# Third and fourth stretch of the second-level products joined, and two more such products, in a Winograd-tiled decoder layer

## The chip, the cores and the metric

The kernel runs on one core of one Trainium2 chip. The metric is the device time of one execution in microseconds (us), and lower is better. The time before is a median of three runs.

## The reference, cut to what matters

One layer of a hybrid decoder over 1024 rows of 1024 numbers, all in float32:

```python
h = rms_norm(x, norm_mix_g)
proj = einsum('bsd,dc->bsc', h, w_in)            # 1024 x 9232 weights
q, k, v, z_a, gk_low, cb, cc, xc, z_c, g_a, g_c = split(proj)
gk = log_sigmoid(gk_low @ w_gk2 + b_gk) / 16
o  = gla_chunked(q, k, v, gk)                     # gated linear attention, chunks of 64
y_a = (rms_norm(o) * silu(z_a)) @ w_branch_a
u   = causal_dwconv(cc * xc, conv_w)              # three taps
y_c = (cb * u * silu(z_c)) @ w_branch_c
merged = sigmoid(g_a + b_ga) * y_a + sigmoid(g_c + b_gc) * y_c
x = x + merged @ w_out
x = x + sigmoid(rms_norm(x) @ w_ple_gate) * (p @ w_ple_proj)
return rms_norm(x, norm_final_g)
```

Nearly all of the work is products of 1024 x 1024 operands. The ones that matter here are h with the columns of q and k, and h with the columns of cc, xc, z_c and cb (the convolution branch).

## The kernel before, in words

**Products.** Every large product is tiled by Winograd's form of Strassen's method: two by two blocks, seven block products (numbered k = 0 to 6) in place of eight. A `Cell` is one such tile: 256 columns of weights against all of h, out as four blocks of 128 x 512. The names are q0, k0, q1, k1 (two heads each) and cc0 to cc3, xc0 to xc3, zc0 to zc3, cb0 to cb3. Each block product has four steps of contraction, and in each step float32 is made of three passes (`mm3`): the operand is split into a rounded part, "hi", and the rest, "lo", and TensorE computes hi·hi, hi·lo and lo·hi. So one block product is 12 matmuls of 128x512. ScalarE makes the hi parts (CAST) and VectorE the lo parts (a subtraction). The prepared weights live in a ring of `RING` = 6 hi and 6 lo buffers.

A cell holds three PSUM banks: X, Y and V. X takes products 0 and 3, V takes 1 and 5, Y begins as a copy of X (ScalarE) and takes 2, then 4, then 6. Cells run in pairs, the first on banks m0 to m2 and the second on m3 to m5, in the order 0, 1, 2, 3, 5, 4, 6, each number for both cells in turn. The finished blocks go to the cell's consumer: `q_cons` and `k_cons` multiply them by exponentials of the decays into a tile `Q` or `kk` and store that; the convolution's consumers gate them.

**Second level.** A `Deep` takes one block product, the same k of both cells of a pair, and tiles these two again by the same method: seven products of two contraction steps, each of 6 matmuls of 128x256, in place of 2 x 12 matmuls of 128x512. It runs in four stretches: the first is 6 matmuls (operand A into the left half of the first cell's bank, copied by ScalarE to the left half of the second cell's), the second is 12 (operand S, both banks), the third is 6 (operand T, the second bank's left half), the fourth is 18 (A and T into the first bank, then B into the second). Between the second and the third stretch, and between the third and the fourth, 256 columns of PSUM are added to other halves by VectorE, with the help of tiles `dw` that ScalarE copies out. The right operands, quarter sums of h, are called `turned0` (for k=0) and `turned1` (k=1) and are loaded once each; the fourth of them is written over a quarter of h's own tile.

Names such as zc1cb10 read: the pair zc1 and cb1, k = 0. A last letter A, S, T or B with hi or lo is the operand of the Deep.

**What sets the order.** `line_up` writes one list of the products of all pairs, and puts the stretches of a pair's Deeps into the list between the last products of the pair before. TensorE follows this list word for word; only attention's matmuls are slipped in. Everything else is recorded first (`Flow.note`) and then put in order by a planner (`put_in_order`), which takes for each engine the ready instruction with the earliest due time; `nc.hurry` makes the due time earlier by so many microseconds. The order is then fixed: each engine, and SyncE's queue of DMAs, works through its own list without overtaking.

**The places of the change.** Before, k = 0 is second-level in the pairs q0k0, q1k1 and all eight convolution pairs (two for each of the four groups), and k = 1 in all convolution pairs but the first, cc0xc0. q0k0 is special (`joined`): its first-level products 1 and 5 come ahead of the Deep, and product 2 begins a bank of its own, which `join` adds to X later. The pool `tq` holds `turned0`, the pool of the convolution stage (`vp`) held `turned1`. `Q` and `kk` have two buffers each. The rest of the kernel (embedding product, v and z_a, gates, attention, the three output projections) has no edit of its own, save that its four Deeps of k = 1 use the same code.

## Time and profile before

| | |
|---|---|
| median of three runs | 1063.58 us (1063.55 to 1064.24) |
| the profiled execution | 1063.67 us, its span 1061.9 us |
| TensorE matmul | 1052.7 us busy, 99% of the span, 5223 instructions |
| VectorE | 937.3 us busy, 88% |
| ScalarE | 671.1 us busy, 63% |
| DMA | 287.53 MB, 271 GB/s on average |
| granted TensorE clock | 0.999 |

The stage of q and k runs from about 227 to 310 us of the span and the convolution's from there to about 600 us. Matmuls are pipelined: the record of one 128x512 matmul is about 0.39 us long, but the next starts 0.23 us later, so prices here are taken from start to start. A row of the timeline has the start, the length, the engine, the source line (always that of the helper, 508), the operation, out<-in, shapes, and in brackets the idle time ahead of it with what ended it.

### The profile page before, as it was taken

The numbers are of one execution on the slowest core, as the hardware profiler recorded it, in microseconds if no ns is written. First come the engines' busy times: TensorE is split into PE (matmuls) and PEld (weight loads), VectorE is DVE, ScalarE is ACT, GpSimd is POOL, SyncE is SP. The second block draws the span as 40 slices with busy tenths as digits, with TensorE's granted clock in tenths as the row PEclk, the third lists the DMA queues.
The fourth block names the chain that finished last, engine by engine and source line by source line (L and its number), as shares of the span: only waits on it lengthen the run. The fifth ranks groups of instructions, "written<-read, shape, count | busy, mean of one in ns | idle before, by whom it ended". The sixth has DMA issues, their size and how long they took to land.

```text
span 1061.9 us, 16352 instructions
## 1 busy us (share of the span) xinstructions
PE 1052.7 (99%) x5223; PEld 894.0 (84%) x5223; DVE 937.3 (88%) x1595; ACT 671.1 (63%) x1282; POOL 52.0 (5%) x83
## 2 busy tenths in 40 slices
PE   9999999999999999999999999999999999999997
PEld 7888887888888888888888899988888888888886
DVE  6899869989988889889889897997999989899897
ACT  6867765776555556567566486776856545456655
POOL 0000000000000000000000011210000000012221
PEclk9999999999999999999999999999999999999999
DMA  9997679878877766876869789988686979799963
GB/s 320 335 362 242 229 250 343 302 252 289 279 216 242 262 215 197 269 251 223 293 221 324 247 258 333 326 265 324 214 295 215 324 218 325 245 325 326 318 214 143
DMA packets 182726, 287.53 MB, mean 271 GB/s; under 512 B 16112, under 2 KB 84976, under 8 KB 180208
## 3 DMA queue, kind: packets, MB, share of 16 engines
q1 hardware_dynamic: 182496, 286.23, 79.5%
q8 instruction: 41, 0.67, 0.3%
q14 instruction: 45, 0.37, 0.1%
q10 hardware_dynamic: 144, 0.26, 0.1%
HBM read 183.14 MB, written 103.28 MB: 270 GB/s over the span
## 4 chain that ended last, share of the span: by engine, by line
PE 97%; DVE 1%; ACT 1%; DMA 0%; issue 0%; POOL 0%; POOLq 0%; SPq 0%; DVEq 0%
PE pe L508 2%; PE op L508 2%; PE zY L508 2%; PE j0Y L508 1%; PE vY L508 1%; PE zV L508 1%; PE j1V L508 1%; PE j1X L508 1%; PE j0V L508 1%; PE j0X L508 1%; PE kv L508 1%; PE ga0Y L508 1%; PE ga2Y L508 1%; PE xc2Y L508 1%; PE cc2Y L508 1%; PE cb1Y L508 1%
## 5 line engine op out<-in xcount | busy, mean ns | idle before, releaser
L508 DVE SCALAR_TENSOR_TENSOR u<-t,vec,u 128x512 f32<-128x512 f32 x32 | 23.9, 754 | 1.6 <-ACT u L508 1.5
L508 DVE TENSOR_TENSOR wt<-wt 128x256 f32<-128x256 f32 (+1 forms) x48 | 24.5, 511 | 0.1
L508 ACT ACTIVATE junk<-x 128x512 bf16<-128x512 f32 (+1 forms) x30 | 18.0, 600 | 10.0 <-DVE x L508 9.7
L508 POOL TENSOR_SCALAR rg<-ms 128x1 f32<-128x1 f32 x8 | 10.2, 1273 | 259.1 <-ACT junk L508 259.0
L508 POOL MEMSET t<- 128x2 f32 x8 | 0.8, 100 | 402.9 <-PE xc0V L508 210.1
L508 ACT ACT_TABLE_LOAD x13 | 16.7, 1283 | 0.9 <-PEq L2321 0.7
L508 ACT ACTIVATE og<-op,or 128x256 f32<-128x256 f32 x32 | 13.4, 474 | 4.2 <-DVE szl L508 2.1
L508 ACT ACTIVATE wt<-wt,vec 128x256 f32<-128x256 f32 x32 | 14.1, 499 | 1.4 <-DVE s L508 0.8
L508 ACT ACTIVATE junk<-op 128x256 bf16<-128x256 f32 x32 | 12.3, 383 | 2.1 <-PE op L508 2.0
L508 POOL TENSOR_SCALAR or<-oms 128x2 f32<-128x2 f32 x16 | 7.9, 494 | 115.7 <-ACT junk L508 115.7
L508 POOL TENSOR_TENSOR or<-or,consts 128x2 f32<-128x2 f32 x16 | 13.5, 842 | 1.3
L508 ACT ACTIVATE u<-t,vec 128x512 f32<-128x512 f32 x16 | 11.6, 723 | 3.0 <-DVE t L508 3.0
L508 ACT ACTIVATE oq<-oq,vec 128x512 f32<-128x512 f32 x20 | 13.4, 717 | 0.0
L508 PE MATMUL op<-v,aTh 128*128 128x256 f32 x64 | 12.9, 284 | 0.0
L508 PE MATMUL pe<-wpehi,pThi 128*128 128x512 f32 x32 | 12.6, 394 | 0.2 <-ACT pThi L508 0.2
L508 DVE TENSOR_TENSOR s<-y,s 128x512 f32<-128x512 f32 x16 | 11.0, 688 | 2.0 <-ACT s L508 1.8
L508 PE MATMUL pe<-wpelo,pThi 128*128 128x512 f32 x32 | 12.7, 397 | 0.0
L508 DVE STREAM_TRANSPOSE oT<-szl 128x256 f32<-128x256 f32 x32 | 12.6, 425 | 0.0
L508 PE MATMUL pe<-wpehi,pTlo 128*128 128x512 f32 x32 | 12.0, 389 | 0.0
L508 ACT CAST S<-S 128x512 fp32r<-128x512 f32 x14 | 8.6, 617 | 5.2 <-PE op L508 4.6
L508 DVE TENSOR_TENSOR x<-x,pe 128x512 f32<-128x512 f32 (+1 forms) x18 | 11.2, 630 | 0.3
L508 DVE SCALAR_TENSOR_TENSOR hq<-hq,vec,rt 128x512 f32<-128x512 f32 x16 | 11.3, 745 | 0.0
(4335 smaller groups left out, 4398.5 us busy)
## 6 DMA issues: line engine op xcount, KB each, us to landing
wtd<-wt SPq DMA_DIRECT2D x88, 128.0 KB, 3.0
wt<-in_wb_dram SPq DMA_DIRECT2D x16, 512.0 KB, 5.3
vsd<-vs SPq DMA_DIRECT2D x16, 512.0 KB, 4.4
v<-vsd SPq DMA_DIRECT2D x16, 512.0 KB, 5.4
vraw<-in_wv_dram SPq DMA_DIRECT2D x28, 256.0 KB, 4.9
wgq<-wtd SPq DMA_DIRECT2D x7, 1024.0 KB, 6.3
zraw<-in_wv_dram SPq DMA_DIRECT2D x20, 256.0 KB, 4.6
uq<-ud SPq DMA_DIRECT2D x5, 1024.0 KB, 7.7
```

The source lines that it names most:

```text
L508: o.call(*[place(a) for a in o.args], **{k: place(a) for k, a in o.kw.items()})
```

## The change

It has five parts.

1. Two more Deeps: k = 1 in the pair q1k1 and in cc0xc0.
2. `line_up` places them otherwise. In a convolution pair there were seven stretches of 128x256 matmuls with other products between; now the fourth stretch follows the third at once, in both Deeps, which leaves five. The same goes for the other pairs of q, k and convolution.
3. In a Deep, one `dw` copy in place of two: ScalarE copies the first bank's right half; VectorE adds it to the second bank's left half, once into the first bank's right half (after the second stretch) and once into the second bank's right half (after the third). These three instructions get 6 us of hurry.
4. q0k0 loses `join`: its order is now the Deep's first stretch, products 1 of both, 5 of the first, the second stretch, 5 of the second, third and fourth stretch, then 3, 2, 4, 6. Y is copied from X after the fourth stretch. Whichever of product 2 and product 5 comes last adds them (`finish`).
5. Memory: `Q` and `kk` share three buffers instead of two each; `turned1` moves to a new pool `tq1`, open from the q and k stage on, and is loaded there; the loads of `turned0` are all recorded at the start.

```diff
-        def join(self):
-            self.c12 = self.taken("u2", self.X)
-            tt(self.c12, self.Y, self.c12, op=ALU.add)
-            nc.scalar.copy(self.Y, self.c12)
+        def finish(self):
             tt(self.c12, self.V, self.c12, op=ALU.add)
             self.cons(0, 1, self.c12)
...
                 self.product(4, self.a[:, right], False)
                 self.product(2, self.b[:, left], False)
-                self.d = [self.pool.tile([P, 256], F32, tag=f"dw{n}", name=f"{a.name}{self.k}dw{n}") for n in range(2)]
-                nc.scalar.copy(self.d[0], self.b[:, left])
-                nc.scalar.copy(self.d[1], self.a[:, right])
-                tt(self.a[:, right], self.a[:, right], self.d[0], op=ALU.add)
+                self.d = self.pool.tile([P, 256], F32, tag="dw", name=f"{a.name}{self.k}dw")
+                nc.hurry = 6.0
+                nc.scalar.copy(self.d, self.a[:, right])
+                tt(self.a[:, right], self.b[:, left], self.d, op=ALU.add)
+                nc.hurry = 0.0
             elif k == 2:
                 self.product(1, self.b[:, left], False)
-                tt(self.b[:, right], self.b[:, left], self.d[1], op=ALU.add)
+                nc.hurry = 6.0
+                tt(self.b[:, right], self.b[:, left], self.d, op=ALU.add)
+                nc.hurry = 0.0
...
-                for n, m in enumerate((3,5,7,8)):
+                for n, m in enumerate((0,4,6,7)):
...
-                for m, (k, n, left) in enumerate(((0, 0, 5), (0, 1, 4), (0, 2, 3), (0, 3, 2), (1, 0, 2), (1, 1, 1), (1, 2, 0))):
+                for m, (k, n, left) in enumerate(((0, 0, 4), (0, 1, 3), (0, 2, 2), (0, 3, 2), (1, 0, 2), (1, 1, 1), (1, 2, 0), (1, 3, 0))):
                     todo.insert(at - left + m, (g[0].deep[k], n))
-                own.insert(1, (g[0].deep[1], 3))
...
-                Q = qp.tile([P, NP, 4, CH], F32, tag="Q", name=f"Q{nm}", bufs=2)
+                Q = qp.tile([P, NP, 4, CH], F32, tag="Qk", name=f"Q{nm}", bufs=3)
...
-            for g in convs[1:] if k else pairs(qks) + convs:
+            for g in (pairs(qks)[1:] if k else pairs(qks)) + convs:
                 Deep(g, k, turned[k], tq)
...
-            c.prods, c.joined = [1, 5, 2, 3, 4, 6], True
+            c.prods, c.joined = [1, 5, 3, 2, 4, 6], True
```

In the lists as built, TensorE has 48 matmuls of 128x512 fewer (3949 to 3901) and 84 of 128x256 more (1194 to 1278). VectorE has 14 additions or subtractions of 128x256 more (221 to 235); ScalarE 17 copies of 128x256 fewer (64 to 47), two casts of 128x512 and two of 128x256 more, and two loads of its function table fewer (13 to 11).

The first place is TensorE at the third stretch of zc1cb10, which writes the left half of cb1's bank X (its last three matmuls head each piece). Before:

```order
L508 MATMUL cb1X<-turned0h,zc1cb10Thi 128x256
L508 MATMUL cb1X<-turned0l,zc1cb10Thi 128x256
L508 MATMUL cb1X<-turned0h,zc1cb10Tlo 128x256
L508 MATMUL xc1Y<-h4hi,xc1hi 128x512
L508 MATMUL xc1Y<-h4lo,xc1hi 128x512
L508 MATMUL xc1Y<-h4hi,xc1lo 128x512
```

And now:

```order
L508 MATMUL cb1X<-turned0h,zc1cb10Thi 128x256
L508 MATMUL cb1X<-turned0l,zc1cb10Thi 128x256
L508 MATMUL cb1X<-turned0h,zc1cb10Tlo 128x256
L508 MATMUL zc1X<-h0hi,zc1cb10Ahi 128x256
L508 MATMUL zc1X<-h0lo,zc1cb10Ahi 128x256
L508 MATMUL zc1X<-h0hi,zc1cb10Alo 128x256
```

The product 4 of xc1, 12 matmuls, stood between the third and the fourth stretch; now the fourth stretch begins at once. Its last six matmuls write cb1's left half again, after VectorE has read it.

The second place is VectorE at that reading, the addition `cb1X<-cb1X,zc10dw`. Before:

```order
L508 TENSOR_TENSOR zc1cb11S_4677<-zc1T_4608,cb1T_4651 128x256
L508 TENSOR_TENSOR qs_3_4529<-qs_3_4529 128x2x128
L508 TENSOR_TENSOR cc1s_4471<-cc1Y,cc1s_4471 128x512
L508 TENSOR_TENSOR cb1X<-cb1X,zc10dw_4640 128x256
L508 SCALAR_TENSOR_TENSOR u_0_4683<-t_0_1_4056,vec,u_0_4683 128x512
```

And now:

```order
L508 TENSOR_TENSOR zc1cb11S_4776<-zc1T_4664,cb1T_4697 128x256
L508 TENSOR_TENSOR zc1cb11S_4781<-cb1T_4697 128x256
L508 TENSOR_TENSOR zc1cb11Alo<-zc1T_4664,zc1cb11Ahi 128x512
L508 TENSOR_TENSOR cb1X<-cb1X,zc10dw 128x256
L508 TENSOR_TENSOR zc1cb11S_4781<-zc1cb11S_4781,zc1T_4664 128x256
```

The addition now stands right behind `zc1cb11Alo`, the lo part of the next Deep's operand A, which itself needs ScalarE's cast `zc1cb11Ahi`.

The third place is ScalarE at q0k0, at the copy that begins the bank q0Y. Before:

```order
L508 CAST q1k10Ahi<-q1raw_2629 128x512
L508 COPY q0u_2795<-q0X 128x512
L508 COPY k0u_2807<-k0X 128x512
L508 ACTIVATE kk_0_2812<-cd_0_2693 128x4x2x64
L508 ACTIVATE kk_0_2812<-c_0_2671 128x4x64
L508 COPY q0Y<-q0u_2795 128x512
```

And now:

```order
L508 CAST q0hi<-q0T_2604 128x512
L508 CAST k0hi<-k0T_2610 128x512
L508 ACTIVATE kk_0_2617<-cd_0_2654 128x4x2x64
L508 COPY q0Y<-q0X 128x512
L508 CAST q1k10Ahi<-q1raw_2642 128x512
L508 COPY k0Y<-k0X 128x512
```

The copy reads q0X itself, and product 3 of q0, which follows the fourth stretch at once, adds into q0X.

More of the change, by code (lines that the diff above doesn't have):

```diff
@@ L828, in run @@
                 self.c22 = self.taken("s5", self.V)
-            elif k == 2 and self.joined:
-                self.Y = bank(self, 1)
-                self.product(2, self.Y, True)
-                if self.X is not None:
-                    self.join()
             elif k == 2:
@@ L836, in run @@
                 self.c12 = self.taken("u2", self.Y)
+                if self.summed:
+                    self.finish()
                 if self.halves:
@@ L844, in run @@
                 self.product(5, self.V, False)
+                self.summed = True
                 if self.c12 is not None:
-                    tt(self.c12, self.V, self.c12, op=ALU.add)
-                    self.cons(0, 1, self.c12)
+                    self.finish()
             elif k in (4, 6) and self.halves:
@@ L940, in run @@
                 self.product(6, self.b[:, left], False)
+                nc.hurry = 0.0
                 for c, t in ((a, self.a), (b, self.b)):
@@ L946, in run @@
                         c.X = t
-                    if c.joined:
-                        if c.Y is not None:
-                            c.join()
-                    elif 1 not in c.deep:
+                    if 1 not in c.deep:
                         c.Y = bank(c, 1)
@@ L954, in run @@
                         c.after(self.k)
+                nc.hurry = 0.0
     def line_up(groups):
@@ L978, in line_up @@
                 at = len(todo)
-                for n in range(3):
-                    todo.insert(at - 3 + 2 * n, (g[0].deep[0], n))
-                own.insert(1, (g[0].deep[0], 3))
+                for n, left in enumerate((3, 2, 1, 0)):
+                    todo.insert(at - left + n, (g[0].deep[0], n))
             elif g[0].deep:
@@ L1657 @@
     tq = phase("tq", [ph["v"]])
-    with phase("qk", [ph["v"]], tq) as qp:
+    tq1 = phase("tq1", [ph["v"]], tq)
+    with phase("qk", [ph["v"]], tq1) as qp:
         ex = lambda o, i_, sg: act(o, i_, AF.Exp, scale=sg / 16.0)
@@ L1814, in convolve @@
         def convolve():
-            weave(quarters(1), 1)
             weave(parts(), 16)
             weave(weights(vp, pieces[3:], 7, 60.0), 10)
-        weave(quarters(0), 1)
+        for _ in quarters(0):
+            pass
+        weave(quarters(1), 4)
         convs[0][0].begin = convolve
@@ L1939 @@
     ycs = [Cell(f"yc{c}", "B", W[f"yc{c}"], ures, None) for c in range(4)]
-    with phase("att", [ph["conv"]], tq) as ap:
+    with phase("att", [ph["conv"], tq1], tq) as ap:
         trim = ap.tile([P, P], I32, name="trim")
```

8 lines of the change are left out of this document (4 added, 4 removed).

## The prediction

> **What bounds the kernel now.** I read the page first: the busy shares, the granted clock, the chain that ended last.
>
> ```profile
> PE 1052.7 (99%) x5223; PEld 894.0 (84%) x5223; DVE 937.3 (88%) x1595; ACT 671.1 (63%) x1282; POOL 52.0 (5%) x83
> PEclk9999999999999999999999999999999999999999
> PE 97%; DVE 1%; ACT 1%; DMA 0%; issue 0%; POOL 0%; POOLq 0%; SPq 0%; DVEq 0%
> ```
>
> TensorE is busy for 99% of the span at full clock, and 97% of the chain is TensorE. So the time is TensorE's list, and an edit counts by how it changes that list or makes it wait. A busy share of matmuls can hide short waits, since their records overlap; so I took the two stages that the change touches from the windows view (busy us of PE, PEld, DVE, ACT, POOL, then clock, DMA share and GB/s), and then TensorE's rows from start to start.
>
> ```profile
> 226.96:310.00 83.04, 83.04 (x425) 71.12 (x424) 76.39 (x153) 50.02 (x98) 0.00 (x0) 1.00 0.85 269
> 310.00:330.00 20.00, 20.00 (x94) 16.72 (x93) 12.63 (x21) 9.87 (x20) 0.20 (x2) 1.00 0.88 290
> ```
>
> In q and k (227 to 310 us) VectorE is idle for 6.7 us and ScalarE for 33; in the next 20 us VectorE is idle for 7.4. Now TensorE's rows in q and k: the first matmul of six blocks, and one that comes 45 wide matmuls after the sixth.
>
> ```profile
> 264.18 0.28 PE L508 MATMUL k1X<-turned0h,q1k10Thi 128*128 128x256 f32 x1
> ...
> 264.89 0.40 PE L508 MATMUL k0Y<-h6hi,k0hi 128*128 128x512 f32 x1
> ...
> 267.63 0.39 PE L508 MATMUL q1V<-h1hi,q1hi 128*128 128x512 f32 x1
> ...
> 270.36 0.28 PE L508 MATMUL q1X<-h0hi,q1k10Ahi 128*128 128x256 f32 x1
> ...
> 272.51 0.40 PE L508 MATMUL k1V<-h1hi,k1hi 128*128 128x512 f32 x1
> ...
> 275.25 0.39 PE L508 MATMUL q1Y<-h2hi,q1hi 128*128 128x512 f32 x1
> ...
> 285.45 0.39 PE L508 MATMUL k1X<-h3hi,k1hi 128*128 128x512 f32 x1
> ```
>
> A wide matmul (128x512) costs (285.45 - 275.25) / 45 = 0.2267 us, a narrow one (128x256) (272.51 - 270.36) / 18 = 0.1194. Twelve wide ones behind a narrow stretch take 272.51 to 275.25 = 2.74 us (264.89 to 267.63 likewise), against 12 x 0.2267 = 2.72: a return from narrow to wide costs about 0.02.
>
> **The two more Deeps, and fewer stretches.** TensorE loses 48 wide matmuls and gains 84 narrow ones: -48 x 0.2267 + 84 x 0.1194 = -10.88 + 10.03 = -0.85 us. In the list, q, k and convolution have 62 blocks of wide matmuls before and 49 now: 13 returns fewer, -13 x 0.02 = -0.26. Together -1.11 us, all of it on the bounding engine, with nothing beside it that could hide it.
>
> [...]
>
> **The work that the Deeps add elsewhere.** VectorE gets 14 operations of 128x256 more:
>
> ```profile
> 241.62 0.43 DVE L508 TENSOR_TENSOR q0X<-q0X,q00dw 128x256 f32<-128x256 f32 x1
> 241.95 0.42 DVE L508 TENSOR_TENSOR q1k10S<-q1raw,k1raw 128x256 f32<-128x256 f32 x1
> ...
> 264.85 0.69 DVE L508 TENSOR_TENSOR k1lo<-k1T,k1hi 128x512 fp32r<-128x512 f32 x1 [0.17 <-ACT k1hi L508]
> ```
>
> They cost 0.33 us each from start to start (the first two rows), so 4.6 us, against the 14.1 us (6.7 + 7.4) idle above. The third row shows the cover: `k1lo` is done at 265.5, and k1's product 1, which needs it, begins at 272.51, 7 us later. ScalarE's copies fall by 17. Cost on the path: nothing as long as that lead lasts; without any idle time and lead it would be the 4.6 us.
>
> **The joint of third and fourth stretch.** This is the edit that can cost. Before, at least one whole product (2.72 us) stood between the two in q1k1 and the convolution pairs; now the third stretch's six matmuls into the second cell's left half are followed by twelve narrow ones (1.43 us) and then by six that add into that same left half, which VectorE must have read by then. Behind the waiting matmuls the rest of TensorE's list is queued, so every bit of lateness is lost time. The trace has such joints already: in ga2ga3 and in q0k0.
>
> ```profile
> 651.37 0.28 PE L508 MATMUL ga3V<-turned2h,ga2ga31Tlo 128*128 128x256 f32 x1
> ...
> 652.81 0.28 PE L508 MATMUL ga2V<-h1hi,ga2ga31Tlo 128*128 128x256 f32 x1
> 653.03 0.39 PE L508 MATMUL ga3V<-h1hi,ga2ga31Bhi 128*128 128x256 f32 x1
> 653.26 0.28 PE L508 MATMUL ga3V<-h1lo,ga2ga31Bhi 128*128 128x256 f32 x1
> ```
>
> ```profile
> 651.95 0.69 DVE L508 TENSOR_TENSOR szl<-og,szl 128x512 f32<-128x512 f32 x1
> 652.56 0.42 DVE L508 TENSOR_TENSOR ga3V<-ga3V,ga21dw 128x256 f32<-128x256 f32 x1
> ...
> 243.67 0.43 DVE L508 TENSOR_TENSOR k0X<-k0X,q00dw 128x256 f32<-128x256 f32 x1 [0.51 <-PE k0X L508]
> ```
>
> ```profile
> 243.35 0.28 PE L508 MATMUL k0X<-turned0h,q0k00Tlo 128*128 128x256 f32 x1
> ...
> 244.91 0.28 PE L508 MATMUL k0X<-h0hi,q0k00Bhi 128*128 128x256 f32 x1
> ```
>
> In q0k0 VectorE was free: the addition starts 243.67 - 243.35 = 0.32 us after the third stretch's last matmul started, ends at 0.75, and the B matmul comes on time at 1.56. In ga3 VectorE was inside `szl`: the addition started at 1.19, ended at 1.61, and B came 0.05 later, at 1.66. From 652.81 to 653.26 it takes 0.45 us where two narrow matmuls take 0.24: 0.21 lost. So the addition may start up to about 1.07 us after the last T matmul: 0.75 us of delay is free, more than the 0.60 of one wide operation ahead of it, less than two.
>
> What stands ahead of it now? In eight of the nine second-level products of k = 0 that get this joint new, the lo part of the next Deep's A, which waits for ScalarE's cast, which waits for the ring buffer that the wide product before the third stretch sets free. Such a cast and lo part, with that product's last matmul:
>
> ```profile
> 374.91 0.39 PE L508 MATMUL cb0Y<-h4hi,cb0lo 128*128 128x512 f32 x1
> ```
>
> ```profile
> 375.16 0.62 ACT L508 CAST cc1xc11Ahi<-cc1T 128x512 fp32r<-128x512 f32 x1 [1.62 <-PE cb0Y L508]
> ```
>
> ```profile
> 375.93 0.69 DVE L508 TENSOR_TENSOR cc1xc11Alo<-cc1T,cc1xc11Ahi 128x512 fp32r<-128x512 f32 x1
> ```
>
> Count from the wide product's end, E = 374.91 + 0.23 = 375.14: the lo part starts at E + 0.79, the addition behind it at E + 1.39 and ends at E + 1.82. B is due at E + 0.72 (third stretch) + 1.43 = E + 2.15 and wants the end by E + 2.10: 0.28 us to spare. So an ordinary joint is free, and one with a second hold-up ahead costs up to the 0.21 of ga3. There are 18 new joints (nine for k = 0, nine for k = 1). Bounds: 0 and 18 x 0.21 = 3.8 us. I take 0.3, near the lower end, as VectorE's row nearest to the new order leaves room and the additions get hurry.
>
> The same edit could give something back: the ga3 joint also gets the hurry, up to -0.21; I take 0.
>
> **The copy that begins q0Y.** In q0k0, product 3 of q0 follows the fourth stretch at once and adds into q0X, and the copy q0Y<-q0X must be done first. q0X is complete six narrow matmuls (0.72 us) before that product. Prices: ScalarE's release and a wide copy.
>
> ```profile
> 239.17 0.28 PE L508 MATMUL q0X<-turned0h,q0k00Slo 128*128 128x256 f32 x1
> ```
>
> ```profile
> 239.49 0.37 ACT L508 COPY q00dw<-q0X 128x256 f32<-128x256 f32 x1 [0.32 <-PE q0X L508]
> ...
> 245.62 0.58 ACT L508 COPY q0u<-q0X 128x512 f32<-128x512 f32 x1
> ```
>
> From q0X's last matmul 0.32 to the copy, 0.58 for it, 0.05 back: 0.95, against 0.12 + 0.72 = 0.84. So 0.11 us is lost at the least, and 0.10 for the restart as in ga3. ScalarE has `kk`'s exponential just ahead in its order, which adds up to another 0.5. Bounds 0.2 and 0.8; I take 0.4, nearer to the lower end, since the copy waits in the order for that one exponential only.
>
> **The start of q and k.** The Deep's operands now come first in the ring, so VectorE does A, S, T and B of q0k0 before `q0lo`.
>
> ```profile
> 219.98 0.68 DVE L508 TENSOR_TENSOR j641lo<-zT,j641hi 128x512 fp32r<-128x512 f32 x1
> 220.58 0.69 DVE L508 TENSOR_TENSOR vbase<-j6X,vbase 128x512 f32<-128x512 f32 x1
> ...
> 226.96 0.39 PE L508 MATMUL q0V<-h1hi,q0hi 128*128 128x512 f32 x1
> ```
>
> Between `j641lo` and `q0lo` stand 11 wide operations and one narrow: 219.98 + 12 x 0.60 + 0.33 = 227.5 to start, 228.2 to end. TensorE wants it with the third matmul behind the first stretch: 226.96 + 0.72 + 0.45 = 228.1. Bounds 0 and 0.3; I take 0.1. `turned0` is wanted earlier too:
>
> ```profile
> 226.79 0.58 SPq L508 DMA_DIRECT2D turned0h<-tqd_0h  x1
> ...
> turned0h<-tqd_0h SPq DMA_DIRECT2D x1, 256.0 KB, 4.9
> ```
>
> Issued at 226.8 it lands 4.9 us later, at 231.7, and the second stretch now starts at 226.96 + 0.72 + 3 x 2.72 = 235.8: 4 us of cover, so no cost; the change would have to delay the load by as much.
>
> **Sum.** -1.11 + 0.3 + 0.4 + 0.1 = -0.3 us. The profiled execution (1063.67) would come to 1063.4. It lies 0.09 above the median, so the median comes to 1063.3.
>
> **Rivals.** First, *all gain, no wait*: every joint and the copy find their engines free but for the 0.2 of the copy, and ga3's 0.21 goes: -1.11, so 1062.5; with the copy free too, 1062.3. For it: q0k0's joint, on time with 0.75 to spare. Against it: the copy's 0.95 against 0.84.
>
> Second, slower: *the addition is late at every joint*. If a second wide operation, 0.60, gets in ahead at each one, the addition ends at E + 2.42 and B loses 0.32 us; at some 0.30 over 18 joints that is +5.4, so 1063.58 - 1.11 + 5.4 = 1067.9. It decides from 0.18 us per joint on (3.2 us in all). For it: in ga3 it happened, with VectorE 88% busy. Against it: it must happen nearly everywhere. [...]
>
> Third, *the shared buffers*: `Q` and `kk` now come free after three consumers and not four, that is one product, 2.72 us, sooner wanted.
>
> ```profile
> ACT Q L508 <- DMA qkd<-Q: 2.1, 2, 1.7
> ...
> ACT kk L508 <- DMA qkd<-kk: 1.0, 1, 1.0
> ...
> qkd<-Q SPq DMA_DIRECT2D x8, 512.0 KB, 4.2
> ```
>
> ScalarE waited for such stores already (the first two rows, from the waits of 227 to 320 us); a store lands after 4.2 us. Two waits that outlast everything by 1.5 us (4.2 - 2.7) would give +3.0 - 0.3: 1066.3. Against it: ScalarE has 33 us idle there, and the casts behind the wait lead TensorE by many us. DMA, at 0.85 of its share, also takes the 2 MB of `turned1` earlier.
>
> That the change doesn't do what it says is no rival: TensorE's list has the 48 and 84.
>
> **How the numbers follow.** A measurement of this kernel tells about 0.2%, 2.1 us, from no change. Forecast (new waits of 0.3 to 2.2 us, 1062.8 to 1064.7): 0.76, no change. All gain: 0.11, no change as well, since even 1.3 us is under the bound. Late additions: 0.07, slower. Buffers: 0.04, half of it slower. Something unseen that gives over 2.1 us: 0.02. So faster 0.02, same 0.89, slower 0.09. The range takes in the forecast, the all-gain case and a little of the buffers' case: 1062.2 to 1065.0.
>
> **What would show it.** Right: blocks of 18 and 24 narrow matmuls merged into 24 and 30; TensorE's rows at the k = 0 and k = 1 joints without gaps over 0.2 us; a gap of 0.2 to 0.6 us ahead of q0X<-h3hi near 243 us. Wrong: gaps at most B matmuls, waits of TensorE on `cb1X` and its like in every pair, or casts that wait for `qkd` stores with TensorE idle behind them; and a time under 1061.4 or over 1065.7.

## The result and the profile after

The changed kernel takes 1065.89 us (median of 22 runs, 1064.56 to 1067.82), the kernel before 1064.01 in the same sets of runs (22 runs, 1063.41 to 1064.96). The ratio is 1.0018, with a 95% interval of 1.0012 to 1.0025: 1.9 us slower. That is just inside the 0.2% within which the prediction spoke of no change, but the interval excludes that there is no difference, and 1065.89 lies above the forecast range (1062.2 to 1065.0). Of the 2.6 us between forecast and result, 0.43 is the kernel before itself, whose 22 runs lie that much above the three shown earlier; 2.2 is the change. The spread from lowest to highest has also grown, from 1.5 to 3.3 us. Among the experiments' runs below, two single executions stand far out (1508.69 us of the kernel before, 3577.39 us of x6) and are left out of the ratios. Two executions of the changed kernel were profiled, one near its fast end (1064.80, span 1062.8) and one near its slow end (1067.14, span 1065.1).

Busy time and chain of the page, changed kernel:

```profile
PE 1052.5 (99%) x5259; PEld 894.9 (84%) x5259; DVE 941.8 (89%) x1609; ACT 666.7 (63%) x1267; POOL 49.0 (5%) x83
PE 94%; DVE 3%; ACT 2%; issue 1%; DMA 1%; POOL 0%; SPq 0%; POOLq 0%; DVEq 0%; ACTq 0%
```

TensorE's share of the chain is 94%, before 97%: there are now waits on VectorE and ScalarE that end last. Where they are is told by TensorE's waits (engine and line, what it waited for, us in total, times, longest). Two rows are new, the rest is as before:

```profile
PE cc0Y L508 <- ACT cc0Y L508: 0.5, 1, 0.5
...
PE q0X L508 <- ACT q0Y L508: 0.2, 1, 0.2
```

The copy `q0Y` was foreseen, `cc0Y` was not. Smaller waits than these hide in the overlap of the records, so I again took TensorE's rows from start to start and counted as a gap what a step takes beyond 0.2267 us (wide) or 0.1194 (narrow). Gaps in us, by place:

| | q0k0 with the start | end of q and k, with cc0xc0 | rest of the convolution | sum |
|---|---|---|---|---|
| changed, first profile | 0.78 | 0.91 | 0.40 | 2.09 |
| changed, second profile | 0.80 | 2.06 | 0.87 | 3.73 |

Five first starts in the three traces give the other side of the account:

| us | before | changed, first | changed, second |
|---|---|---|---|
| to j6Y, the last block ahead of q and k | 219.02 | 218.89 | 219.62 |
| j6Y to xc0Y<-h6hi | 125.75 | 126.73 | 127.88 |
| xc0Y to zc3Y<-h6hi | 252.43 | 252.56 | 253.02 |
| zc3Y to gc1Y<-h6hi | 122.39 | 122.32 | 122.32 |
| gc1Y to the last matmul | 334.41 | 334.41 | 334.41 |

In the first profile q and k grew by 0.98 with 1.69 of gaps, so the shorter list gave 0.71 there; the convolution grew by 0.13 with 0.40 of gaps, so 0.27. Together about 1.0 us of the 1.11 came. The gaps took 2.1 to 3.7. So the account is -1.0 + 2.1 = +1.1 for the first profile (measured 1064.80 against 1063.67, +1.13) and -1.0 + 3.7 = +2.7 for the second (measured 1067.14, +3.47). Of the 0.8 us that the second account misses, 0.60 lies ahead of j6Y (219.62 against 219.02), outside the stages that the change touches, and the rest outside the span (1067.14 - 1065.1 against 1063.67 - 1061.9).

**The end of q and k.** Here is the wait for `cc0Y`, followed back in the timeline of the changed kernel:

```profile
299.31 0.68 DVE L508 TENSOR_TENSOR Q<-q1s,Q 128x512 f32<-128x512 f32 x1
304.86 0.42 DVE L508 TENSOR_TENSOR Q<-Q,dcs 128x256 f32<-128x256 f32 x1
305.34 0.52 SPq L508 DMA_DIRECT2D qkd<-Q  x1
310.05 0.62 ACT L508 CAST cc0hi<-cc0raw 128x512 fp32r<-128x512 f32 x1 [1.97 <-PE k1Y L508]
310.57 0.63 ACT L508 ACTIVATE Q<-c 128x512 f32<-128x512 f32 x1
312.08 0.68 DVE L508 TENSOR_TENSOR Q<-q1Y,Q 128x512 f32<-128x512 f32 x1
312.92 0.28 PE L508 MATMUL xc0V<-h1hi,cc0xc01Blo 128*128 128x256 f32 x1
313.13 0.57 ACT L508 COPY cc0Y<-cc0X 128x512 f32<-128x512 f32 x1
313.75 0.50 PE L508 MATMUL cc0Y<-h2hi,cc0hi 128*128 128x512 f32 x1 [0.55 <-ACT cc0Y L508]
314.08 0.39 PE L508 MATMUL cc0Y<-h2lo,cc0hi 128*128 128x512 f32 x1
```

and the same steps before:

```profile
302.40 0.68 DVE L508 TENSOR_TENSOR Q<-q1Y,Q 128x512 f32<-128x512 f32 x1
306.86 1.20 SPq L508 DMA_DIRECT2D qkd<-Q  x2
310.18 0.59 ACT L508 COPY cc0Y<-cc0X 128x512 f32<-128x512 f32 x1
```

cc0's new bank Y is the bank of q1Y, so the copy waits until VectorE has read q1Y. Read the first fence backwards: that reading (312.08) needs the exponentials of a new `Q` tile (310.57). They need a buffer, which the store at 305.34 frees. That store waits for the multiplication by `dcs`, which stands at 304.86 although its input was done at 299.99: for the most part operands of cc0xc0's new second-level product stand ahead of it in VectorE's order. The store lands 3.2 us after its issue, at 308.56, so the buffer is free 2.0 us before the exponentials start. What they wait for last is their turn on ScalarE, behind the cast `cc0hi` (310.05), which stands 1.97 us for TensorE. So it is the fixed order that sets 310.57; that the planner put the exponentials behind that cast because the buffer comes free late is argued, not shown. Before, q1Y was read 9.7 us earlier.

VectorE is what became tight there. The windows of the changed kernel (PE, PEld, DVE, ACT, POOL, clock, DMA share, GB/s):

```profile
226.96:310.00 83.04, 82.87 (x452) 71.91 (x451) 75.77 (x153) 48.88 (x94) 0.00 (x0) 1.00 0.89 290
310.00:330.00 20.00, 19.45 (x98) 16.37 (x97) 16.72 (x32) 12.20 (x24) 0.20 (x2) 1.00 0.67 208
264.00:318.00 54.00, 53.45 (x300) 46.70 (x299) 52.58 (x109) 32.57 (x67) 0.10 (x1) 1.00 0.75 236
```

and the last one in the kernel before:

```profile
264.00:318.00 54.00, 54.00 (x270) 45.96 (x269) 49.96 (x100) 28.64 (x58) 0.20 (x2) 1.00 0.79 247
```

The first window would have told nothing: VectorE is idle for 7.3 us in it, 6.7 before. In the second its idle time falls from 7.4 to 3.3, and in the 54 us around the end of the stage it has 1.4 us left of 4.0, with nine instructions more. Two of the nine are weight preparation (`wt`) for a later stage: its third piece now starts at 290.6, where it started at 279.3 before.

**The joints.** One that is late, in the convolution (VectorE ahead of it, then TensorE):

```profile
488.08 0.74 DVE L508 SCALAR_TENSOR_TENSOR u<-t,vec,u 128x512 f32<-128x512 f32 x1
488.74 0.68 DVE L508 TENSOR_TENSOR zc2cb21Alo<-zc2T,zc2cb21Ahi 128x512 fp32r<-128x512 f32 x1
489.34 0.42 DVE L508 TENSOR_TENSOR cb2X<-cb2X,zc20dw 128x256 f32<-128x256 f32 x1
```

```profile
487.96 0.28 PE L508 MATMUL cb2X<-turned0h,zc2cb20Tlo 128*128 128x256 f32 x1
...
489.40 0.28 PE L508 MATMUL zc2X<-h0hi,zc2cb20Tlo 128*128 128x256 f32 x1
489.82 0.39 PE L508 MATMUL cb2X<-h0hi,zc2cb20Bhi 128*128 128x256 f32 x1
```

The addition starts 489.34 - 487.96 = 1.38 us after the last T matmul. The prediction allowed 1.07; it is 0.31 over, and the B matmul starts 0.42 behind its predecessor in place of 0.12: 0.30 lost, and 0.10 more in the restart (the next one starts 0.22 behind it, at 490.04, in place of 0.12). Two wide operations stood ahead, `u` and `Alo`. So at this joint the model holds to a hundredth, but the lateness occurs at two of the 18 joints in the first profile (the other, the k = 1 joint of cc0xc0, loses 0.10) and at four in the second, not at all or none.

**The copy and the start.** The copy as forecast:

```profile
242.89 0.58 ACT L508 COPY q0Y<-q0X 128x512 f32<-128x512 f32 x1
243.07 0.28 PE L508 MATMUL k0X<-h0hi,q0k00Blo 128*128 128x256 f32 x1
243.52 0.50 PE L508 MATMUL q0X<-h3hi,q0hi 128*128 128x512 f32 x1 [0.17 <-ACT q0Y L508]
```

The last narrow matmul starts at 243.07, the wide one 0.45 later where 0.12 is a plain step; with the gaps of the next two steps it is 0.44. And ahead of q and k something not foreseen:

```profile
218.16 0.69 DVE L508 TENSOR_TENSOR j640lo<-zT,j640hi 128x512 fp32r<-128x512 f32 x1 [0.62 <-ACT j640hi L508]
218.77 0.68 DVE L508 TENSOR_TENSOR j6c<-j6Y,vbase 128x512 f32<-128x512 f32 x1
219.50 0.19 PEld L508 LDWEIGHTS j6Y<-j670hi,qs6h 128*128 128x128 f32 x1 [0.42 <-DVE j6c L508]
```

Before, the addition `j6c` stood ahead of `j640lo` and began at 218.18; now it stands behind it, and TensorE waits for it (0.27 us lost). Late q0lo adds 0.07.

### The profile page after: what moved, and what is told of

It is laid out like the page before. It is cut to its first block, busy times and chain, and to the rows that moved or that the text cites. A ratio compares the mean times of both kernels' runs of the same rounds, so it can differ in the third digit from the quotient of the medians.

```text
span 1062.8 us, 16423 instructions
## 1 busy us (share of the span) xinstructions
PE 1052.5 (99%) x5259; PEld 894.9 (84%) x5259; DVE 941.8 (89%) x1609; ACT 666.7 (63%) x1267; POOL 49.0 (5%) x83
## 4 chain that ended last, share of the span: by engine, by line
PE 94%; DVE 3%; ACT 2%; issue 1%; DMA 1%; POOL 0%; SPq 0%; POOLq 0%; DVEq 0%; ACTq 0%
PE pe L508 2%; PE op L508 2%; PE zY L508 2%; PE j0Y L508 1%; PE vY L508 1%; PE zV L508 1%; PE j1V L508 1%; PE j1X L508 1%; PE j0V L508 1%; PE j0X L508 1%; PE kv L508 1%; PE cc0Y L508 1%; PE j6Y L508 1%; PE ga2Y L508 1%; PE ga0Y L508 1%; PE ga1Y L508 1%
## 5 line engine op out<-in xcount | busy, mean ns | idle before, releaser
L508 DVE SCALAR_TENSOR_TENSOR S<-S,dds,kv 128x256 f32<-128x256 f32 x24 | 10.5, 473 | 0.8 <-PE kv L508 0.8
```

What stands on the lines that cost most here:

```text
L508: o.call(*[place(a) for a in o.args], **{k: place(a) for k, a in o.kw.items()})
```

## Experiments

Of each experiment: the edit to the changed kernel (x6: to the kernel before), then what was expected on record, what was measured, and what follows. Ratios are to the kernel before in the same set of runs; its medians lay between 1063.96 and 1064.25. Gaps are read from each experiment's one profile.

**x1, x2: the weights' preparation out of q and k, then own buffers.** VectorE also prepares weights for a later stage (`wt`) between its work for q and k. x1 moves that into the convolution; x2 does too, which makes room for own buffers of `Q` and `kk`, so x1 is its control.

```diff
-        weave(weights(qp, pieces[:3], 3, 30.0), 1)
-            weave(weights(vp, pieces[3:], 7, 60.0), 10)
+            weave(weights(vp, pieces, 7, 60.0), 10)
```

```diff
-                Q = qp.tile([P, NP, 4, CH], F32, tag="Qk", name=f"Q{nm}", bufs=3)
+                Q = qp.tile([P, NP, 4, CH], F32, tag="Q", name=f"Q{nm}", bufs=2)
```

> The kernel after, with one thing moved: the first part of the value's weight preparation, which is woven into the q/k stage, goes to the convolution stage, where the rest of it already is. It frees memory in the q/k stage and leaves the three shared buffers of Q and kk as they are; it is the control for the next run. Buffer theory (the 1.9 us are mostly waits for the three shared buffers): the waits stay, +1.5 to +2.2 us against the kernel before. Order theory (q0k0's new order and the joints): the same, +1.5 to +2.2. If it comes to +1 or less, the woven preparation itself had been in the way of VectorE or ScalarE, and neither theory is needed for that part.

> The control's move, and Q and kk with two buffers each again, as in the kernel before. Buffer theory: the wait of 0.71 + 0.10 us ahead of cc0Y<-h2hi goes, and with it what differs from run to run: median +0.0 to +0.9 us against the kernel before, 1.0 to 1.9 us under the control, and single runs closer together (1.5 us rather than 3.3 us from lowest to highest). Order theory: within 0.4 us of the control, the gap of 0.8 us at cc0Y still there, since VectorE's and ScalarE's backlog there would come from the shorter time between k1Y and cc0Y.

x1: 1068.04, ratio 1.0036 [1.0023, 1.0050]; x2: 1067.85, 1.0033 [1.0020, 1.0045]. x1 is slower than either theory allowed (+3.8 us over before). x2 lies 0.2 us under it, as the order theory had it, but the gap at cc0Y, which that theory kept, is gone. The gaps at cc0xc0 are gone in both, and the convolution loses 2.6 us (x1) and 3.9 (x2), nearly all at its joints. With VectorE relieved at the end of q and k, nothing is lost there, with shared or own buffers; with VectorE loaded in the convolution, joints are lost there.

**x6: the kernel before with the shared buffers alone.**

> The kernel before, with nothing changed but the buffers of Q and kk: three in common in place of two each. TensorE's list is that of before, so what it loses is the price of the shared buffers alone. Buffer theory: +0.8 to +2 us, with new waits of ScalarE for qkd stores and TensorE waiting at the end of q and k. If the buffers matter only together with the shorter distances that the new stretches leave, or not at all: within 0.4 us of before.

1063.82, ratio 0.9998 [0.9989, 1.0007]. ScalarE does wait for the stores (its waits between 227 and 320 us):

```profile
ACT kk L508 <- DMA qkd<-Q: 3.9, 3, 2.5
```

TensorE waits for none of it. The shared buffers cost nothing by themselves.

**x5: the changed kernel again**, to see what differs between its executions.

> The kernel after, unchanged, for a second profile and for its time beside the three others of this set. Its first profile was one of its shortest executions (1064.8, median 1065.9). Waiting-for-stores theory (waits of ScalarE for the landing of qkd stores change from run to run and carry the rest of the loss): the wait ahead of cc0Y<-h2hi is longer than 0.7 us here, 1.5 to 3 us, with ScalarE waiting for qkd<-kk or qkd<-Q before it, and nearly all that this execution takes longer lies at 300 to 320 us. Other theory (small waits everywhere): the difference is spread over the stages. Median +1.5 to +2.3 us.

1066.27, ratio 1.0018 [1.0009, 1.0027]. The profile is the second one above. At the end of q and k:

```profile
292.23 0.69 DVE L508 TENSOR_TENSOR wt<-wt 128x512 f32<-128x512 f32 x1 [0.80 <-DMA wt<-in_wb_dram]
296.85 0.42 DVE L508 TENSOR_TENSOR kk<-kk,dcs 128x256 f32<-128x256 f32 x1
299.85 0.52 SPq L508 DMA_DIRECT2D qkd<-kk  x1
304.63 0.63 ACT L508 ACTIVATE kk<-cd 128x512 f32<-128x512 f32 x1 [1.98 <-DMA qkd<-kk]
305.80 0.69 DVE L508 TENSOR_TENSOR cc0xc01Tlo<-cc0xc01S,cc0xc01Thi 128x512 fp32r<-128x512 f32 x1 [0.79 <-ACT cc0xc01Thi L508]
314.11 0.39 PE L508 MATMUL xc0V<-h1hi,cc0xc01Bhi 128*128 128x256 f32 x1 [0.39 <-DVE xc0V L508]
315.63 0.50 PE L508 MATMUL cc0Y<-h2hi,cc0hi 128*128 128x512 f32 x1 [0.55 <-ACT cc0Y L508]
```

It begins with a load of weights: VectorE stands 0.80 us for it, since it took 7.0 us from issue to landing, 5.0 in the first profile. What is behind it in VectorE's order comes later by that much, and the k = 0 joint of cc0xc0 loses 0.59 us at 302.94. The store at 299.85 has its data from 297.3 on, SyncE's queue is at other transfers, and it lands after 4.7 us (4.6 in the first profile, so the store itself isn't slower). ScalarE's exponential waits 1.98 us for it to land (1.06 in the first profile), the cast of the operand T stands behind that exponential, VectorE waits 0.79 for the cast (0.31), and the k = 1 joint of cc0xc0 loses 0.65, the copy 0.81. So the same order loses 0.9 or 2.1 us here.

The other profiles agree that a late load picks this joint. In x3, x8 and x15 VectorE stands 2.13, 0.99 and 1.05 us for the same load, and the k = 0 joint of cc0xc0 loses 1.33, 1.06 and 0.64; in the first profile and in x7, x9, x12, x13 and x14 it stands 0.19 at most, and that joint is on time. The same holds at the k = 0 joint of the next pair, cc1xc1: it loses 0.80 us here, 0.67 in x9 and 0.56 in x14, and each time VectorE has stood 1.15, 0.69 and 0.91 us for a load of `y` some 8 us earlier; without that wait it is on time. The stretches apart hide such waits: in x17 VectorE stands 1.2 to 1.8 us for transfers at three places of the convolution, and TensorE loses nothing. Why a load takes longer in one execution than in another is open, and no experiment moves a load alone.

**x3, x8: q0k0's first-level products between the stretches.** They are to give the copy `q0Y` cover; x8 leaves the first stretch where it is.

```diff
-                for n, m in enumerate((0,4,6,7)):
+                for n, m in enumerate((1,3,5,6)):
```

```diff
-                for n, m in enumerate((0,4,6,7)):
+                for n, m in enumerate((0,3,5,6)):
```

> The kernel after, with another place for the first product's stretches in q0k0: the first-level product 1 first, the stretches of product 0 behind products 1, k1, 5 and beside 5's, with k5 behind the last, so that a whole narrow product of k0 lies between q0X's last matmul and the copy's user. Order theory: the three gaps that belong to q0k0 in the profile (0.26 us at j6Y, 0.07 us at q0V, 0.44 us ahead of q0X<-h3hi) go, together 0.77 us: +1.1 us against the kernel before where the kernel after has +1.9. Buffer theory: the same for these 0.8 us at most, and the gap of 0.8 us at cc0Y stays. Joint theory: no change, +1.9. A new gap elsewhere in q0k0 (VectorE at j6Y or at the first copy) would show as less than 0.3 us gained.

> The kernel after, with the second to fourth stretches of q0k0 put one product earlier, so that product 5 of k0 (2.72 us) lies between the fourth stretch and product 3 of q0, which adds onto the copy of q0X; the first stretch stays first. The copy term alone: the gap of 0.44 us ahead of q0X<-h3hi goes, the two at j6Y and q0V stay, and the median falls by 0.4 us against the kernel after. A price that could eat it: stretch two one product earlier finds VectorE with q0k00Slo or k0lo not done (up to 0.7 us, as in the run with the first-level product first).

x3: 1067.71, ratio 1.0032 [1.0019, 1.0044]; x8: 1067.82, 1.0035 [1.0022, 1.0048]. Neither was expected to be slower than the changed kernel; both are, x8 by 1.55 us in the same set. In x8 the copy's gap is gone, and cc0xc0's gaps are 2.32 us (3.44 in x3, whose ScalarE waits 2.73 for a store of `kk`):

```profile
302.99 0.38 PE L508 MATMUL xc0X<-h0hi,cc0xc00Bhi 128*128 128x256 f32 x1 [0.80 <-DVE xc0X L508]
```

TensorE arrives 0.4 us sooner at a place where VectorE sets the pace, and waits there. But VectorE also stands for the load of weights here (0.99 us in x8, 2.13 in x3), and the order around it shifts, so how much of the loss is TensorE's earlier arrival alone isn't shown. What is shown is that the wait removed upstream gained nothing while that place was late.

**x4: the stretches back in their old places**, with the two new products kept.

```diff
-                for m, (k, n, left) in enumerate(((0, 0, 4), (0, 1, 3), (0, 2, 2), (0, 3, 2), (1, 0, 2), (1, 1, 1), (1, 2, 0), (1, 3, 0))):
+                for m, (k, n, left) in enumerate(((0, 0, 5), (0, 1, 4), (0, 2, 3), (0, 3, 2), (1, 0, 2), (1, 1, 1), (1, 2, 0))):
...
+                own.insert(1, (g[0].deep[1], 3))
```

> The kernel after, with the places of the second-level stretches in pairs that have two such products put back to what they were (the third stretch ahead of the fourth's place by one product, so that no addition falls between two adjacent stretches). Joint theory (third and fourth stretch side by side cost 0.4 us or more in sum): the gap of 0.40 us at cb2X<-h0hi goes, and if the added stretch itself brings less than that the time falls to +0.8 to +1.5 us. Buffer theory and order theory: +1.5 to +2.2 us as in the kernel after, perhaps 0.3 us more for the returns between wide and narrow that come back (some 13 of 0.02 us); the gap at cc0Y stays unless the old places also lengthen the time from k1Y to cc0Y, in which case it is smaller than 0.5 us.

1068.42, ratio 1.0041 [1.0028, 1.0053], slower than expected. The convolution's joints lose nothing now, which clears the old places; but cc0Y's wait is 2.53 us and q0k0's gaps are 1.34. The joints were not the larger part of the loss.

**x7, x12: one new product left out.** In x7 it is q1k1's, in x12 cc0xc0's. In both, the plain product of that pair then reads a quarter of h that has been replaced by a sum, so that part of the output is not the reference's.

```diff
-            for g in (pairs(qks)[1:] if k else pairs(qks)) + convs:
+            for g in convs if k else pairs(qks) + convs:
```

```diff
-            for g in (pairs(qks)[1:] if k else pairs(qks)) + convs:
+            for g in pairs(qks)[1:] + convs[1:] if k else pairs(qks) + convs:
```

> The kernel after without the second-level product of k = 1 in q1 and k1; that of cc0 and xc0 stays. TensorE's list gets 24 wide matmuls more and 42 narrow ones fewer: +0.43 us, and one or two returns, +0.03. Theory that VectorE's backlog from this product (seven narrow operations, and casts due earlier) delays Q and kk: the gap at cc0Y goes and the spread with it, so +0.5 to +1.2 us against before. Theory that cc0's own product brings it (its stretches shorten the way from k1Y to cc0Y): +1.9 to +2.5 us, the gap still there.

> The kernel after without the second-level product of k = 1 in cc0 and xc0 (these read a quarter of h that is replaced by then, so their output isn't the reference's); that in q1 and k1 stays. TensorE's list gets 24 wide matmuls more and 42 narrow ones fewer, +0.43 us. Theory that this product is the cause (its operands are due while VectorE finishes Q and kk, and its joint and the copy cc0Y come 4 us sooner after k1Y): the gaps at 300 to 316 us go, the median falls to +0.4 to +1.2 us. Theory that q1k1's own product fills VectorE: gaps of over 1 us stay, +1.9 to +2.5.

x7: 1065.42, ratio 1.0013 [1.0004, 1.0023], with cc0Y's gap still 0.74. x12: 1064.54, 1.0004 [0.9995, 1.0013], no gap at cc0xc0, and a spread of 0.91 us, although TensorE's list is 0.43 longer (half of the 0.85). cc0xc0's product is the one whose operands fall due when `Q` and `kk` are not yet finished.

**x9: a third of the weights' preparation moved.**

```diff
-        weave(weights(qp, pieces[:3], 3, 30.0), 1)
+        weave(weights(qp, pieces[:2], 3, 30.0), 1)
```

> The kernel after, with two weight pieces woven into the q/k stage in place of three; the third, which VectorE reaches at 290 us there and whose load it waited for in three of the profiles (0.8, 1.0 and 2.1 us), goes to the convolution stage. Theory that VectorE's backlog at the end of q and k is the cause, with landings of DMA moving it from run to run: the gaps at 300 to 316 us (0.8 us in the first profile of after, 2.1 in the second) go, and the median falls by 0.8 to 1.5 us against after, to +0.5 to +1.3 against before, less what the piece costs in the convolution (up to 0.9 us, a third of what three pieces cost there in the run that moved all). Theory that the stores of Q and kk alone are the cause: ScalarE's waits for them stay, and the median within 0.4 us of after.

1066.28, ratio 1.0021 [1.0012, 1.0030]. The joint at cc0xc0 is on time, the copy cc0Y still loses 0.74, and the convolution loses 1.49 (the piece now falls there). Less work on VectorE is not enough for cc0Y: the order of its chain counts.

**x10, x11: the stores of `Q` and `kk` issued by GpSimd** (x11: with x9 too), so that SyncE's other transfers can't hold them up. The store of `kk` is edited likewise.

```diff
-                store(qkd[hp][i][:, :, j, 0:2 * P], Q.rearrange("p n s t -> p n (s t)"))
+                nc.gpsimd.dma_start(qkd[hp][i][:, :, j, 0:2 * P], Q.rearrange("p n s t -> p n (s t)"))
```

> The kernel after, with the stores of Q and kk issued by GpSimd, which is idle there, and no longer by SyncE, where they stood behind the stores of the weight pieces and of the transposed parts (a store of kk whose data was done at 297.3 was issued at 299.9 in the second profile of after). Store theory (ScalarE's wait for the landing of qkd starts the backlog): the waits of ScalarE for qkd at 302 to 305 us go, the gaps at the joint of cc0V and at cc0Y with them, and the median falls by 0.8 to 1.5 us. Theory that VectorE's backlog is there anyway (weight load late, q1k1's and cc0's products side by side): ScalarE's waits go but the gaps at 300 to 316 us stay over 1 us; within 0.5 us of after.

> The kernel after with both of the two edits beside it: two weight pieces in the q/k stage, and the stores of Q and kk issued by GpSimd. If the two waits are two parts of one backlog, it gains what the better of the two gains and up to 0.5 us more; only the gaps of q0k0 (0.8 us) and single joints of the convolution are left: -0.3 to +0.8 us against before. If neither is the cause it stays at +1.5 or more.

x10: 1083.98, ratio 1.0181 [1.0167, 1.0195]; x11: 1085.31, 1.0199 [1.0185, 1.0213]. No expectation allowed for this. In x10 GpSimd issues stores late (one of `kk`, done at 252.09, at 257.16), others land late (one of `Q`, issued at 295.25, after 7.8 us, with ScalarE waiting 5.83 for it), and TensorE stands for 3.3, 5.8 and 2.6 us (the last section has two of the waits). As a test of SyncE's queue it says nothing, but it shows that later stores do reach TensorE by this chain.

**x13, x14, x15: the order of the consumers.** x13 gives hurry only to the multiplication by `dcs` and to the store behind it; x14 to the whole consumer, 6 us from its first exponential on; x15 is x13 with x8's order.

```diff
+                nc.hurry = 8.0
                 tt(Q[:, :, 1, :], Q[:, :, 3, :], dc[:, :, 0:1].to_broadcast([P, NP, CH]), op=ALU.mult)
+                nc.hurry = 40.0
                 store(qkd[hp][i][:, :, j, 0:2 * P], Q.rearrange("p n s t -> p n (s t)"))
+                nc.hurry = 0.0
```

```diff
+                nc.hurry = 6.0
                 ex(Q[:, :, 0:4:3, :], c4, -1.0)
...
+                nc.hurry = 40.0
                 store(qkd[hp][i][:, :, j, 0:2 * P], Q.rearrange("p n s t -> p n (s t)"))
+                nc.hurry = 0.0
```

The same lines stand in `kk`'s consumer.

> The kernel after with nothing but another order on VectorE, ScalarE and SyncE: the last multiplication of each Q and kk and its store get hurry, so that the three buffers come free sooner (in the kernel after the multiplication that completes a Q stood 5 us behind its input, in both profiles). TensorE's list, the work and the buffers are the same. Order theory (the shared buffers come free late because the planner puts Q's last multiplication behind cc0's operands): the exponentials of Q run at 302 to 306 us rather than 310 to 312, the gap of 0.8 us at cc0Y goes, and the median falls by 0.6 to 1.5 us against after, to +0.4 to +1.4 against before. Amount theory (VectorE is full from 264 to 317 us, so what is put ahead pushes back what follows): other gaps of the same size at the joints of cc0, and the median within 0.4 us of after.

> As the run beside it, but with hurry on the whole consumer of Q and kk, exponentials and multiplications too, by less (6 where the last multiplication had 8). Order theory: the same gain or more (0.6 to 1.8 us under after). Amount theory: cc0's operands slip and the joints of cc0 show it, 0 to 1 us over after.

> As the first of these three, and product 5 of k0 between the fourth stretch and q0's product 3, which took away the gap of 0.44 us ahead of q0X<-h3hi but gave it all back at cc0 in the run with that edit alone. Order theory: with the buffers free sooner nothing is given back, so 0.4 us better than the run beside it. Amount theory: VectorE is the bound of that stretch, so that TensorE, 0.44 us earlier, only waits longer at cc0: no better than the run beside it.

x13: 1065.34, ratio 1.0012 [1.0004, 1.0021], spread 0.94 us. With the same buffers, products and preparation of weights, and only the order changed, cc0xc0 has no gap (VectorE doesn't stand for the load of weights here, as in the first profile, which lost 0.81 at the copy):

```profile
303.89 0.62 ACT L508 ACTIVATE Q<-c 128x512 f32<-128x512 f32 x1
312.99 0.28 PE L508 MATMUL xc0V<-h1hi,cc0xc01Blo 128*128 128x256 f32 x1
313.11 0.40 PE L508 MATMUL cc0Y<-h2hi,cc0hi 128*128 128x512 f32 x1
```

The exponential that stood at 310.57 is at 303.89, and cc0Y's matmul follows 0.12 behind. The convolution's joints lose 1.30 here. x14: 1064.86, 1.0011 [1.0002, 1.0020]; gaps 0.57 in q0k0, none at cc0xc0, 0.60 in the convolution. x15: 1065.30, 1.0013 [1.0004, 1.0022]: the copy's gain is spent on a second stretch that now comes a product earlier and waits 0.52 us for the load of `turned0l`; 0.64 is lost at the k = 0 joint of cc0xc0, with VectorE 1.05 behind the load of weights, and 1.2 in the convolution. The copy cc0Y is on time there too.

**x16, x17: the joints, with x14's order of the consumers.** x16 takes the stretches of k = 0 apart again, x17 those of both (with x4's edit).

```diff
-                for m, (k, n, left) in enumerate(((0, 0, 4), (0, 1, 3), (0, 2, 2), (0, 3, 2), (1, 0, 2), (1, 1, 1), (1, 2, 0), (1, 3, 0))):
+                for m, (k, n, left) in enumerate(((0, 0, 5), (0, 1, 4), (0, 2, 3), (0, 3, 2), (1, 0, 2), (1, 1, 1), (1, 2, 0), (1, 3, 0))):
```

> The run with hurry on the whole consumer of Q and kk, and with the third and fourth stretch of k = 0 apart again by one product, as in the kernel before (nine pairs, so nine returns more: 9 x 0.02 = +0.18 us); those of k = 1 stay side by side. Joint theory (what is left of the loss beside q0k0 is the k = 0 joints of the convolution, 0.4 to 0.9 us in a profile, wherever VectorE happens to be late): no gap at a k = 0 joint in the profile, the spread from lowest to highest falls under 1.5 us, and the median to +0.2 to +0.7 us against before. Rival: the stretches begin one product earlier, so cc0's operands are due 2.7 us sooner in the stretch where VectorE is full, and the gaps at 300 to 316 us come back: +1.2 us or more.

> As the run beside it, with the k = 1 stretches in their old places too, the fourth behind the next pair's first product: thirteen returns as in the kernel before (+0.26 us), the two added products stay. Joint theory: no joint gap at all, +0.2 to +0.8 us. The copy cc0Y follows the fourth stretch more closely here (its gap was 2.5 us in the run with the old places alone): if hurry on Q and kk does not cover that, it shows as a gap of over 0.5 us at cc0Y and +1 to +2.5 us.

x16: 1066.47, ratio 1.0019 [1.0010, 1.0028], a partial miss for both theories: the joints of k = 0 are clean, and 1.73 us are lost at k = 1, 1.0 of it where the first stretch waits for its own `Alo` and 0.71 at this joint, behind a `lo` part:

```profile
538.21 0.68 DVE L508 TENSOR_TENSOR cc3lo<-cc3raw,cc3hi 128x512 fp32r<-128x512 f32 x1
538.57 0.28 PE L508 MATMUL cc3V<-h1hi,cc3xc31Tlo 128*128 128x256 f32 x1
538.81 0.43 DVE L508 TENSOR_TENSOR xc3V<-xc3V,cc31dw 128x256 f32<-128x256 f32 x1
539.29 0.38 PE L508 MATMUL xc3V<-h1hi,cc3xc31Bhi 128*128 128x256 f32 x1 [0.45 <-DVE xc3V L508]
```

x17: 1064.16, 0.9999 [0.9990, 1.0008], spread 0.85: no gap in the convolution or at cc0xc0. What is left is 1.34 in q0k0, of it 0.73 for the copy.

**x18: x17 with x8's order of q0k0.**

> As the last run (old places, hurry on Q and kk), and product 5 of k0 between q0k0's fourth stretch and q0's product 3. The only waits that the last run had over the kernel before are q0k0's: 0.28 us at j6Y, 0.05 and 0.28 at q0V, 0.73 ahead of q0X<-h3hi. If TensorE is the bound there again, the 0.73 goes and nothing gives it back: 0.4 to 0.8 us under the last run, 1063.3 to 1063.8, below the kernel before by 0.3 to 0.8 us. Rival: the second stretch of q0k0 comes one product sooner and waits for the load of turned0 (0.5 us in the run with both edits and the new places): within 0.3 us of the last run.

1063.23 (1062.87 to 1064.33), ratio 0.9993 [0.9984, 1.0002]: the first version with the two new products whose median is below that of before (1064.17) by more than a tenth, 0.9 us, though the interval just reaches 1. The copy now has product 5 of k0 in front of it:

```profile
240.56 0.57 ACT L508 COPY q0Y<-q0X 128x512 f32<-128x512 f32 x1 [1.39 <-PE q0X L508]
243.60 0.39 PE L508 MATMUL k0V<-h5hi,k0lo 128*128 128x512 f32 x1
243.83 0.39 PE L508 MATMUL q0X<-h3hi,q0hi 128*128 128x512 f32 x1
```

Only 0.37 us of gaps are left in these stages. The same product behind the copy that changed nothing for the better in x8 shows in the time here, since nothing after it waits any more. Not all of the gain over the kernel before is the change's, though. In the profiles q and k are 0.26 us shorter than before and the convolution is the same, while the stretch from zc3Y to gc1Y, which is not edited, takes 121.97 us in place of 122.39; x6, the kernel before with shared buffers, has 121.97 there as well.

## Why the prediction was wrong

1. *The list, -0.85 and -0.26.* Right: about -1.0 by the stretches of the first profile (0.71 and 0.27).
2. *VectorE's added work at nothing, "as long as that lead lasts".* This step failed. The lead of 7 us was read at `k1lo`, early in the stage; at its end, where the operands of cc0xc0's new product fall due, VectorE went from 4.0 to 1.4 us idle in 54, and the order put those operands ahead of `dcs`. In place of nothing, the end of q and k cost 0.91 us in one profile (0.81 at cc0Y, 0.10 at a joint) and 2.06 in the other, where VectorE had also stood 0.80 us for a load. x12 (product out) and x13 (order only) both bring it to none in their profiles, neither with such a wait. So the order's part, the copy cc0Y, is shown; that the late load causes the rest is inferred from the agreement of the profiles.
3. *The shared buffers, the third rival.* Its mechanism took part, at another place: the wait comes not by the casts that lead TensorE, but by q1Y, whose reading needs a `Q` buffer and whose bank cc0Y needs. The argument "ScalarE has 33 us idle there" was no argument, since idle time in a stage's mean doesn't stand where the wait stands. The buffers alone cost nothing (x6), nor do they with VectorE relieved (x2 against x1).
4. *The joints, +0.3.* The model of one joint was right (0.31 late by its rule, 0.30 lost, and the restart), and the sum was not far off in the convolution: 0.40 and 0.87 in the two profiles. With cc0xc0's own, which point 2 counts, it is 0.51 and 2.1, so for the second profile this term was too small too. The second rival needed all 18; two and four were late. Which ones they are differs between orders (x1, x9, x13, x16) and between executions of one order. At cc0xc0 and cc1xc1 the late ones at k = 0 are those ahead of which VectorE stood for a load, which the prediction left out; what picks the others, as cb2X's, is open.
5. *The copy, +0.4.* Right: 0.44, and x8 and x18 remove it with one product of cover.
6. *The start, +0.1.* It cost 0.34: 0.07 for `q0lo` as foreseen, and 0.27 for `j6c`, which the planner put behind `j640lo`. I had compared the order only where the edits are.
7. *ga3's joint.* Its 0.21 gap is gone, yet the stretch around it is only 0.07 shorter, partly because TensorE's gap at attention's `op` (709 us in the first profile) grew from 0.22 to 0.36; I took 0.
8. *`turned0`, no cost.* Right for this order, and x15 shows how near: one product earlier, and the second stretch waits 0.52 us for `turned0l`.

The grown spread fits the second and fourth points: x12, x13 and x17, without waits at cc0xc0, have spreads of 0.85 to 0.94 us; but x14, with none there in its one profile either, has 2.5 and x18 1.5, and the kernel before itself had 2.1 in the set of x17, so this is not settled.

## What to carry to other kernels

Read the idle time and the lead of an engine where the added work falls due, above all at the end of a stage where one consumer's last tiles meet the next stage's first operands, and not as a stage's mean. When work is added there, follow the chain from the bank or buffer that the next stage wants back through its reader, that reader's buffer and the store that frees it, and look at what the order puts ahead of each link. Work that follows at once, as the joined stretches do, leaves no room for an engine that stands for a load, so look for such waits ahead of each joint and compare several executions. A wait taken away upstream of a place that binds can gain nothing until that place has slack again (x8 against x18), so try such edits together and not only one at a time.

## What the hardware showed that was not expected

In x10, GpSimd's issues of the stores and TensorE's two long waits (timeline, then windows with the granted clock ahead of the DMA share):

```profile
262.59 0.58 PE L508 MATMUL q1X<-turned0h,q1k10Shi 128*128 128x256 f32 x1 [3.33 <-ACT k1X L508]
308.83 0.58 PE L508 MATMUL cc0X<-turned0h,cc0xc00Shi 128*128 128x256 f32 x1 [5.79 <-ACT xc0X L508]
328.96 0.72 POOL L508 DMA_DIRECT2D qkd<-kk  x1 [3.27 <-issue]
332.18 0.72 POOL L508 DMA_DIRECT2D qkd<-kk  x1 [2.51 <-DVE Q L508]
```

```profile
262.00:264.00 2.00, 1.41 (x6) 1.41 (x7) 2.00 (x5) 1.38 (x4) 0.00 (x0) 0.50 0.89 333
...
266.00:268.00 2.00, 2.00 (x6) 1.52 (x6) 2.00 (x6) 0.80 (x2) 0.00 (x0) 0.50 1.01 365
...
270.00:275.00 5.00, 5.00 (x37) 4.71 (x36) 4.98 (x11) 2.62 (x6) 0.00 (x0) 1.00 0.27 98
```

GpSimd's issues of these stores stand at least 3.2 us apart, also where the data is there (the one issued at 260.87, 3.7 us after the last, had its data at 256.75); in the kernel before, SyncE issued two in 1.20 us (the row at 306.86, shown above). And after an idle time of 3.3 us TensorE's granted clock was 0.50 for 6.2 us of work, until 268.8 (the window from 268 to 269 has 0.61, the next one 1.00), so by estimate a wait of 3.3 us cost some 3 us more, half of the 6.2. After the second wait, 5.8 us, matmuls of 128x512 start 0.43 us apart (311.56 and 311.98) and from 313.22 on 0.23 again, so the slow stretch lasted about 4.3 us. Why it was 6.2 us the one time and 4.3 the other isn't shown.

A shorter wait had a small cost of its own too: in the changed kernel, after 0.55 us of idle time, the matmul at 313.75 is 0.50 us long where its like is 0.39, and the next one starts 0.33 behind it in place of 0.23. The granted clock from 313 to 314 us is 1.00 there.
